# A state-space stage reordered: GpSimd products moved to VectorE, half a projection placed later, outputs as full-array matmuls

## The chip, the core and the metric

The kernel runs on one core of one Trainium2 chip. The metric is device microseconds of one execution, the median of three runs. Matmuls are on TensorE (PE in the profile; its weight loads are PEld), elementwise work on VectorE (DVE), ScalarE (ACT) and GpSimd (POOL); SyncE (SP) issues nearly all DMAs.

## The reference

A two-layer decoder trunk over 512 positions and 1024 channels. Layer 0 is an S5 state-space mixer and a SwiGLU feed-forward network (FFN); layer 1 is latent attention and a second FFN. The change touches only the mixer. Its core, cut to what matters:

```python
def s5_mixer(h, w_in, lam_re, lam_im, log_step, b_re, b_im, c_re, c_im, d_skip, w_glu):
    u = (h @ w_in).reshape(bsz, seq, 64, 16)           # 64 groups of 16 channels
    step = jnp.exp(log_step)[:, None]
    decay = jnp.exp(lam_re * step)
    a_re, a_im = decay * jnp.cos(lam_im * step), decay * jnp.sin(lam_im * step)
    ...                                                # br, bi: input weights scaled by f(a, lambda)
    def scan_sequence(u_seq):                          # x[l] = a * x[l-1] + B u[l], 64 complex states a group
        bu_re = jnp.einsum('gnk,lgk->lgn', br, u_seq)
        bu_im = jnp.einsum('gnk,lgk->lgn', bi, u_seq)
        _, _, xr, xi = lax.associative_scan(combine, (ar_seq, ai_seq, bu_re, bu_im), axis=0)
        return jnp.einsum('gkn,lgn->lgk', cr, xr) - jnp.einsum('gkn,lgn->lgk', ci, xi)
    y = lax.map(scan_sequence, u) + d_skip * u
    z = jax.nn.gelu(y)
    val, gate = jnp.split(z @ w_glu, 2, axis=-1)
    return val * jax.nn.sigmoid(gate)
```

## The kernel before

All fp32 products with full-size weights are made from three fp32r matmuls: each operand is split into a rounded high part (ACT copy) and the rest (DVE subtraction). For weights `weights` does this (DMA into `w`, `wh` on ACT L141, `wl` on DVE L142, two buffers for `w`, three for `wh` and `wl`), for activations `split` does. `mm3` issues the three matmuls (L153, L154, L155).

The mixer (`s5_core`) has four parts.

- **Prologue.** x comes in eight row blocks, `w_in` in eight slabs. Each x block is split (`sh`, `sl`) and squared (`xsq`). `project(0, n)` makes the first half of the projection's columns in four PSUM banks of the kind "x" (96 matmuls), `project(1, n)` the second half in the banks "g" (96 more). Meanwhile DVE, POOL and ACT work out decay, angles and their powers on tiles of 128x32 (`exp_exact`, `turns`, `cmul`), and POOL makes the table `counts`, the tile `DI` and sums of squares.
- **Tiles.** The 512 positions are 128 chunks of 4. Eight tiles t of 8 groups each go through `coefs` (weights W and E for tile t+2, on DVE), `turn_u` and `turn_w` (transposes on PE, copied by ACT into `uT`, `WT`), `rotor` (sines and cosines of whole tiles: `allp` and `near` in PSUM, `whole` on DVE, `Sn`, `Cs` on ACT), `taps` (64x64 matmuls, copied by ACT into `Tb`), `scan` (chunk sums on PE L599, then on DVE: `pc`, `qc`, `z`, two scan instructions L610, `xpc`, `xqc`, and the states `X`), and `outputs`: 16 matmuls with `Tb` (L631) and 64 with E and X (L639) on 128x32 and 64x32 parts of the array, GELU on ACT into `zf`, split into `zh`, `zl`. An fp32 matmul shows as two rows in the trace, a transpose as one.
- **GLU columns in the tiles.** `partial(k)` multiplies tile k's split output with four of the 16 column blocks of `w_glu` (12 matmuls into "g").
- **GLU rest.** In `s5`, for m of 2 to 7, 48 matmuls each, then FFN 0 begins.

The code gives a program order and priorities; a scheduler at build time then fixes one order for each engine, and the chip keeps to it: an instruction that waits holds all those behind it on its engine. PSUM has eight banks; the four "x" banks are handed out in turn, so a new user waits for the readers of the use four before.

Of the kernel before, what the change touches and what calls it, by code (L numbers as in the profile page):

```python
# [88 lines left out]
class Trunk:  # L89
# [207 lines left out]
    def s5_core(self, st):  # L297
# [100 lines left out]
        for t in range(NCT):  # L398
# [5 lines left out]
        tt(counts.rearrange("p a b c -> p (a b) c"), self.c("chunk").unsqueeze(1).broadcast_to([P, 3 * PPC, C]),  # L404
           self.c("pairrow").unsqueeze(2).broadcast_to([P, 3 * PPC, C]), M_, g)
# [43 lines left out]
        for o, x, n, signs in ((ArS, Ar, T + 1, (1.0, -1.0)), (AiN, Ai, T + 1, (-1.0, -1.0)), (GrS, Gr, T, (1.0, 1.0)), (GiS, Gi, T, (-1.0, 1.0))):  # L449
# [5 lines left out]
           self.c("kdelta").unsqueeze(1).broadcast_to([P, 2 * NCT, 32]), M_, g)  # L455
# [14 lines left out]
        Tb = [lp.tile([P, 2, 2, T, 2, 16], F32, name=f"Tb{i}") for i in range(NB)]  # L470
        E2 = [lp.tile([P, 4, 2, T + 1, 2, 16], F32, name=f"E{i}") for i in range(NB)]
# [6 lines left out]
        for z in Tb + E2:  # L478
            g.memset(z, 0.0)
# [3 lines left out]
        def evacuate(q):  # L483

            Us[q] = cp.tile([P, 4 * PPC, T, 16], F32, name="U", bufs=3)
            for i in range(T):
                nc.scalar.activation(out=Us[q][:, :, T - 1 - i, :], in_=ups[q // 2][i][:, (q % 2) * 256:(q % 2 + 1) * 256].rearrange("p (a k) -> p a k", k=16),
                                     func=AF.Copy, scale=rs[:, i:i + 1])

        def coefs(t):  # L490
# [5 lines left out]
            def weigh(o, j, n, re, im):  # L496
                def bb(x):
                    return x.unsqueeze(2).broadcast_to([P, 2 * PPC, n, 16])

# [4 lines left out]
                tt(ma, bb(bc[:, j]), gg(re), M_)
                tt(mb, bb(bc[:, j + 1]), gg(im), M_)
                if o is not None:
                    return tt(o, ma, mb, A_)
                for e in range(2):
                    tt(E2[t % NB][:, :, e, :, e], *(m.rearrange("p (a e) j k -> p a e j k", e=2)[:, :, e] for m in (ma, mb)), A_)

# [3 lines left out]
            weigh(None, 2, T + 1, ArS, AiN)  # L514
            coef[t] = {"W": W}

        def rotor(t):

            allp, near = self.ps("x"), self.ps("x")

            def turns_of(o, j, start, stop):
                nc.tensor.matmul(out=o, lhsT=turned[:, t], rhs=counts[:, j].rearrange("p a b -> p (a b)"), start=start, stop=stop)

            turns_of(allp, 2, True, True)
            whole = cp.tile([P, PPC * C], BF16, name="whole", bufs=1)
            v.tensor_scalar(out=whole, in0=allp, scalar1=MAGIC, scalar2=-MAGIC, op0=A_, op1=A_)
            turns_of(near, 0, True, False)
            nc.tensor.matmul(out=near, lhsT=negident, rhs=whole, start=False, stop=False)
            turns_of(near, 1, False, True)
# [9 lines left out]
        def taps(t):  # L539
# [3 lines left out]
            E = E2[t % NB]  # L543
            kps = [self.ps("x") for _ in range(2)]
            for odd in (1, 0):
                for q in range(2):
                    for c in range(2):
                        for e in range(2):
                            for g2 in range(2):
# [5 lines left out]
                                                 rhs=E[h, 2 * q + c, e, 0:(T if odd else T - 1), e],  # L555
                                                 start=odd == 1 and q == 0 and c == 0, stop=odd == 0 and c == 1, skip_group_check=True)
            for g2 in range(2):
                h = slice(64 * g2, 64 * g2 + 64)
                nc.tensor.matmul(out=kps[g2][:, 0:128].rearrange("p (a u k) -> p a u k", a=2, u=T)[:, :, 0:2, :], lhsT=self.c("places")[h],
                                 rhs=DI[h, 2 * t:2 * t + 2].rearrange("p a (u k) -> p a u k", u=2), start=False, stop=True, skip_group_check=True)  # L560
            for g2 in range(2):
                k4 = kps[g2][:, 0:128].rearrange("p (a u k) -> p a u k", a=2, u=T)
                for e in range(2):
                    for ip in range(2):
                        h = slice(64 * e + 32 * ip, 64 * e + 32 * ip + 32)
                        n = 2 * ip + 2
# [52 lines left out]
        def outputs(t):  # L619

            b = t % NB
            uT, E = states.pop(t), E2[t % NB]
            ps_y = self.ps("x")

            def block(g2, q, j):
                return ps_y[64 * g2 + 32 * q:64 * g2 + 32 * q + 32, j * C:(j + 1) * C]

            for j in range(T):
                for q in range(2):
                    for g2 in range(2):  # L630
                        nc.tensor.matmul(out=block(g2, q, j), lhsT=Tb[t % NB][:, q, g2, j].rearrange("p e k -> p (e k)"), rhs=uT[:, q, g2],  # L631
                                         start=j == 0, stop=False, skip_group_check=True)
            for j in range(T):
                for e in range(2):
                    for c in range(2):
                        for q in range(2):
                            for g2 in range(2):
                                h = slice(64 * g2, 64 * g2 + 64)
                                nc.tensor.matmul(out=block(g2, q, j), lhsT=E[h, 2 * q + c, e, 1 + j].rearrange("p e k -> p (e k)"),  # L639
                                                 rhs=X[b][h, c, 2 * e + q], start=False, stop=e == 1 and c == 1, skip_group_check=True)  # L640
# [18 lines left out]
        for k in range(1, 5):  # L659
            tt(sqs[0], sqs[0], sqs[k], A_, g)  # L660
# [475 lines left out]
```

## Time and profile before

| | |
|---|---|
| median of three runs | 1246.48 us (1244.24 to 1248.38) |
| the profiled execution | 1248.45 us, of which the span of its instructions is 1246.7 us |
| mixer, first instruction to the first FFN matmul | 0 to 276.36 us |
| PE busy in the span | 1190.2 us (95%) |
| DVE, ACT, POOL busy in the span | 673.0, 477.9, 150.4 us |
| mean granted TensorE clock | 0.981 of full speed |

The span runs from the first to the last instruction. Busy shares are means over stages with different limits, so the rows further down cut the span at the borders of the mixer's parts. In a timeline row the first number is the start, the second the time that the merged instructions took; overlapping instructions on PE each show their whole duration, so the spacing of starts tells the pace.

### The profile page before, as it was taken

What the parts mean: (1) busy time and instruction counts of PE and PEld (TensorE: products, weight loads), DVE (VectorE), ACT (ScalarE), POOL (GpSimd) and SP (SyncE); (2) the same over time, 40 slices, a digit from 0 to 9 for tenths busy, and PEclk for the clock granted to TensorE, in tenths of its full rate; (3) what the DMA queues carried; (4) which work ended last, traced back from release to release, by engine and by line L of the source; (5) the groups of instructions that cost most, each with busy time, mean ns of one, the idle gap of its engine ahead of it and who ended that gap; (6) DMA issues with size and microseconds to landing.
All of it is one profiled execution on the core that took longest, in us unless ns stands there. A gap on an engine that the chain in (4) does not pass through costs nothing.

```text
span 1246.7 us, 17562 instructions
## 1 busy us (share of the span) xinstructions
PE 1190.2 (95%) x7160; PEld 964.3 (77%) x7160; DVE 673.0 (54%) x1185; ACT 477.9 (38%) x795; POOL 150.4 (12%) x167
## 2 busy tenths in 40 slices
PE   5978889999999999999999898999999999999998
PEld 4856677888888888888878666666888888888887
DVE  8688895456444444333337777854764444443221
ACT  5464444344333323223336666653342232232210
POOL 4400000002000000000142444342100000000000
PEclk8989899999999999999999899999999999999999
DMA  5201011333333333333232011102333333323331
GB/s 194 89 30 36 10 37 36 118 88 96 104 90 96 101 98 89 93 95 104 85 101 61 27 35 42 52 1 85 88 99 101 92 95 102 102 88 100 121 118 47
DMA packets 31904, 101.09 MB, mean 81 GB/s; under 512 B 3664, under 2 KB 4688, under 8 KB 31824
## 3 DMA queue, kind: packets, MB, share of 16 engines
q1 hardware_dynamic: 31680, 99.97, 26.1%
q8 instruction: 56, 0.92, 0.3%
q14 instruction: 24, 0.20, 0.1%
q10 hardware_dynamic: 144, 0.00, 0.0%
HBM read 97.86 MB, written 2.10 MB: 80 GB/s over the span
## 4 chain that ended last, share of the span: by engine, by line
PE 82%; DVE 13%; ACT 3%; issue 2%; POOL 1%; DMA 0%; DVEq 0%; SPq 0%; ACTq 0%
PE ps_ps L153 19%; PE ps_ps L154 19%; PE ps_ps L155 19%; PE ps_s L942 2%; PE ps_x L154 2%; PE ps_x L155 2%; PE ps_x L153 2%; PE ps_a L153 2%; PE ps_a L155 2%; PE ps_a L154 2%; DVE z L610 1%; PE ps_po L979 1%; PE ps_a L927 1%; PE ps_a L959 1%; PE ps_g L154 1%
## 5 line engine op out<-in xcount | busy, mean ns | idle before, releaser
L141 ACT ACTIVATE wh<-w 128x1024 fp32r<-128x1024 f32 (+3 forms) x193 | 191.0, 992 | 554.5 <-PE ps_ps L154 362.1
L142 DVE TENSOR_TENSOR wl<-w,wh 128x1024 fp32r<-128x1024 f32 (+3 forms) x193 | 222.2, 1152 | 213.4 <-ACT wh L141 213.2
L153 PE MATMUL ps_ps<-fh,wh 128*128 128x512 f32 x704 | 274.2, 390 | 0.0
L155 PE MATMUL ps_ps<-fh,wl 128*128 128x512 f32 x704 | 273.4, 389 | 0.0
L154 PE MATMUL ps_ps<-fl,wh 128*128 128x512 f32 x704 | 273.4, 389 | 0.0
L153 PEld LDWEIGHTS ps_ps<-fh,wh 128*128 128x128 f32 x704 | 132.1, 188 | 28.0 <-issue 0.5
L154 PEld LDWEIGHTS ps_ps<-fl,wh 128*128 128x128 f32 x704 | 132.1, 188 | 27.7 <-issue 0.5
L155 PEld LDWEIGHTS ps_ps<-fh,wl 128*128 128x128 f32 x704 | 132.1, 188 | 27.5
L153 PE MATMUL ps_ps<-ah,wh 128*128 128x512 f32 x352 | 136.9, 389 | 0.0
L154 PE MATMUL ps_ps<-al,wh 128*128 128x512 f32 x352 | 136.9, 389 | 0.0
L155 PE MATMUL ps_ps<-ah,wl 128*128 128x512 f32 x352 | 136.9, 389 | 0.0
L263 POOL TENSOR_TENSOR acc<-acc,sq 128x512 f32<-128x512 f32 x21 | 30.6, 1456 | 580.7 <-ACT sq L258 315.8
L720 DVE TENSOR_TENSOR ut<-ps_ps,rstd 128x512 f32<-128x512 f32 x44 | 30.4, 691 | 127.9 <-PE ps_ps L155 127.9
L155 PEld LDWEIGHTS ps_ps<-ah,wl 128*128 128x128 f32 x352 | 66.1, 188 | 13.8
L154 PEld LDWEIGHTS ps_ps<-al,wh 128*128 128x128 f32 x352 | 66.1, 188 | 13.7
L153 PEld LDWEIGHTS ps_ps<-ah,wh 128*128 128x128 f32 x352 | 66.1, 188 | 13.7
L717 DVE TENSOR_TENSOR gt<-ps_ps,rstd 128x512 f32<-128x512 f32 x44 | 30.4, 691 | 82.8 <-PE ps_ps L155 82.7
L950 POOL TENSOR_SCALAR p<-p,sm 128x128 f32<-128x128 f32 (+2 forms) x48 | 45.7, 955 | 68.8 <-DVE sm L948 61.4
L942 PE MATMUL ps_s<-kT,qT 96*128 96x384 f32 (+3 forms) x128 | 46.3, 465 | 1.6 <-ACT p L947 1.6
L947 ACT ACTIVATE p<-ps_s,mx 128x128 f32<-128x128 f32 (+3 forms) x64 | 33.4, 525 | 29.1 <-DVE mx L945 24.9
L168 ACT ACTIVATE ah<-ut 128x512 fp32r<-128x512 f32 x44 | 27.9, 633 | 31.3 <-DVE ut L721 31.3
L945 DVE TENSOR_REDUCE mx<-ps_s 128x1 f32<-128x128 f32 (+3 forms) x64 | 30.4, 484 | 16.5 <-PE ps_s L943 16.2
(383 smaller groups left out, 1767.7 us busy)
## 6 DMA issues: line engine op xcount, KB each, us to landing
w<-w_gu SPq DMA_DIRECT2D x88, 512.0 KB, 3.5
w<-w_down SPq DMA_DIRECT2D x32, 512.0 KB, 3.5
w<-w_glu SPq DMA_DIRECT2D x12, 512.0 KB, 3.5
w<-w_down SPq DMA_DIRECT2D x16, 384.0 KB, 3.0
w<-w_in SPq DMA_DIRECT2D x7, 512.0 KB, 4.1
w<-w_o SPq DMA_DIRECT2D x6, 512.0 KB, 3.5
x<-xT SPq DMA_DIRECT2D x8, 256.0 KB, 6.9
bc<-ssm_bc SPq DMA_DIRECT2D x8, 256.0 KB, 2.8
```

What stands on the lines that cost most here:

```text
L141: nc.scalar.activation(out=wh[:, c], in_=w[:, c], func=AF.Copy)
L142: nc.vector.tensor_tensor(out=wl[:, c], in0=w[:, c], in1=wh[:, c].bitcast(F32), op=ALU.subtract)
L153: nc.tensor.matmul(out=out, lhsT=lh, rhs=rh, start=start, stop=False)
L154: nc.tensor.matmul(out=out, lhsT=lh, rhs=rl, start=False, stop=False)
L155: nc.tensor.matmul(out=out, lhsT=ll, rhs=rh, start=False, stop=stop)
L263: nc.gpsimd.tensor_tensor(out=acc, in0=acc, in1=sq, op=ALU.add)
L717: v.tensor_tensor(out=gt, in0=pss[0], in1=rstd, op=ALU.mult)
L720: v.tensor_tensor(out=ut, in0=pss[1], in1=rstd, op=ALU.mult)
L942: nc.tensor.matmul(out=ps, lhsT=qT[:, i * P:n], rhs=kT[:, 0:n], start=True, stop=False)
L945: v.reduce_max(out=m1, in_=ps, axis=AX.X, negate=True)
L947: nc.scalar.activation(out=pb, in_=ps, func=AF.Exp, bias=m1, accum_out=s1)
L950: eng.tensor_scalar(out=pb, in0=pb, scalar1=s1, scalar2=None, op0=M_)
```

## The change

The diff, cut to its core:

```diff
+        with tc.high_priority():
             load_x(0)
             load_w(0, 2)
             split_x(0)
...
             split_x(6, 7)
         nc.sync.dma_start(out=self.ct, in_=a["consts"])
...
         counts = sp.tile([P, 3, PPC, C], F32R, name="counts")
-        tt(counts.rearrange("p a b c -> p (a b) c"), self.c("chunk").unsqueeze(1).broadcast_to([P, 3 * PPC, C]),
-           self.c("pairrow").unsqueeze(2).broadcast_to([P, 3 * PPC, C]), M_, g)
+        for j in range(3):
+            for i in range(PPC):
+                nc.scalar.activation(out=counts[:, j, i], in_=self.c("chunk"), func=AF.Copy, scale=self.c("pairrow")[:, PPC * j + i:PPC * j + i + 1])
...
-            tt(q[2], ar, bi, M_, g)
-            tt(q[3], ai, br, M_, g)
+            tt(q[2], ar, bi, M_)
+            tt(q[3], ai, br, M_)
             tt(orr, q[0], q[1], S_)
-            tt(oi, q[2], q[3], A_, g)
+            tt(oi, q[2], q[3], A_)
...
-           self.c("kdelta").unsqueeze(1).broadcast_to([P, 2 * NCT, 32]), M_, g)
+           self.c("kdelta").unsqueeze(1).broadcast_to([P, 2 * NCT, 32]), M_)
...
-            weigh(None, 2, T + 1, ArS, AiN)
-            coef[t] = {"W": W}
+            E = cp.tile([P, 2 * PPC, T + 1, 16], F32, name="E")
+            weigh(E, 2, T + 1, ArS, AiN)
+            for g2 in range(2):
+                h = slice(64 * g2, 64 * g2 + 64)
+                nc.scalar.activation(out=Obd[t % NB][h, :, :, g2], in_=E[h, :, 1:], func=AF.Copy)
+            coef[t] = {"W": W, "E": E}
+
+        def whole_turns(t):
+            allp = self.ps("x")
+            turns_of(t, allp, 2, True, True)
+            rotors[t] = cp.tile([P, PPC * C], BF16, name="whole")
+            v.tensor_scalar(out=rotors[t], in0=allp, scalar1=MAGIC, scalar2=-MAGIC, op0=A_, op1=A_)
...
-            for j in range(T):
-                for q in range(2):
-                    for g2 in range(2):
-                        nc.tensor.matmul(out=block(g2, q, j), lhsT=Tb[t % NB][:, q, g2, j].rearrange("p e k -> p (e k)"), rhs=uT[:, q, g2],
-                                         start=j == 0, stop=False, skip_group_check=True)
...
+            for q in range(2):
+                for g2 in range(2):
+                    nc.tensor.matmul(out=ps_y.rearrange("p (q e j g k) -> p q g e j k", q=2, e=2, j=T, g=2)[:, q, g2], lhsT=uT[:, q, g2],
+                                     rhs=Tb[t % NB][:, q, g2].rearrange("p e j k -> p (e j k)"), start=q == 0 and g2 == 0, stop=False, skip_group_check=True)
+            for q in range(2):
                 for e in range(2):
                     for c in range(2):
+                        nc.tensor.matmul(out=ps_y[:, (2 * q + e) * P:(2 * q + e + 1) * P], lhsT=X[b][:, c, 2 * e + q],
+                                         rhs=Obd[b][:, 4 * q + 2 * c + e].rearrange("p j g k -> p (j g k)"), start=False, stop=c == 1, skip_group_check=True)
+            Y = cp.tile([P, T, PPC, 32], F32, name="Y", bufs=1)
+            nc.scalar.activation(out=Y.rearrange("p j a k -> p a j k"), in_=ps_y.rearrange("p (a j k) -> p a j k", a=PPC, j=T), func=AF.Gelu_apprx_tanh)
+            states[t] = Y
+
+        def turn_y(t):
+            Y = states.pop(t)
+            ps_z = self.ps("x")
+            for j in range(T):
+                nc.tensor.transpose(out=ps_z[:, j * C:(j + 1) * C], in_=Y[:, j].rearrange("p a k -> p (a k)"), identity=ident)
             z = self.pair(t, "z")
-            self.split(z[0], z[1], zf)
+            self.split(z[0], z[1], ps_z)
             zs.append(z)
...
         for k in range(1, 5):
-            tt(sqs[0], sqs[0], sqs[k], A_, g)
+            tt(sqs[0], sqs[0], sqs[k], A_)
...
-        for n in range(4):
-            load_w(4 + n)
-            project(1, n)
         coefs(0)
         turn_u(0)
-        taps(0)
         turn_w(0)
-        rotor(0)
-        scan(0)
-        coefs(1)
-        for t in range(1, 4):
+        for t in range(2):
+            whole_turns(t)
+        rotor(0)
+        taps(0)
+        scan(0)
+        rotor(1)
+        coefs(1)
+        rest(0)
+        for t in range(2, 4):
+            whole_turns(t)
             rotor(t)
         for t in range(NCT):
-            for f, d in ((turn_u, 1), (turn_w, 1), (later_u, 0), (scan, 1), (taps, 1), (outputs, 0), (partial, -1), (coefs, 2)):
+            for f, d in ((turn_u, 1), (turn_w, 1), (scan, 1), (taps, 1), (outputs, 0), (coefs, 2), (turn_y, 0)):
...
+            if t == 0:
+                rest(1)
+                rest(2)
+            if t == 1:
+                rest(3)
+                evacuate(2)
...
+            if t >= 3:
+                for k in range(0 if t == 3 else t - 1, t):
+                    partial(k)
```

`rest(n)` loads slab 4 + n of `w_in` and calls `project(1, n)`. `Obd` holds E for two channel groups side by side, with zeros between, so that one full-array matmul with a state tile X as its weights does what eight small ones did; the result has chunks on the partitions, and `turn_y` turns it back by four transposes before it is split. On POOL only the copies into `phs` and the memsets stay in the mixer. The host's rows of `w_glu` change their order with it.

What the built order makes of it, at three places. First ACT at its very start, where it squares, splits and rounds the first x blocks and weight slabs. Before:

```order
L171 ACT_TABLE_LOAD
L171 ACTIVATE sh_88<-x,smalls 128x512
L346 ACTIVATE xsq<-x 128x512
L141 ACTIVATE wh<-w 128x512 x2
L171 ACTIVATE sh_93<-x,smalls 128x512
L346 ACTIVATE xsq<-x 128x512
L141 ACTIVATE wh<-w 128x1024
L171 ACTIVATE sh_105<-x,smalls 128x512
L346 ACTIVATE xsq<-x 128x512
```

and after the change:

```order
L347 ACT_TABLE_LOAD
L347 ACTIVATE xsq<-x 128x512
L141 ACTIVATE wh<-w 128x512 x2
L171 ACTIVATE sh_88<-x,smalls 128x512
L407 ACTIVATE counts<-ctab 128x128 x12
L409 ACTIVATE negident<-ctab 128x128
L171 ACTIVATE sh_93<-x,smalls 128x512
L347 ACTIVATE xsq<-x 128x512
L141 ACTIVATE wh<-w 128x1024
```

The twelve copies for `counts` and `negident`, which read the constants' DMA (`ctab`), now stand ahead of the second x block `sh_93`; on SP the DMAs of `ctab` and of three `bc` tiles have moved ahead of x blocks 1 to 7 (`ctab`, one `bc`, x1, two `bc`, then the second slab).

Second, ACT ahead of the first scan. `U` is the projection's first half, scaled by the rsqrt `rs`; `wh` 128x1024 is a slab of `w_in`. Before:

```order
L487 ACTIVATE U<-ps_x,rs 128x16x16 x8
L141 ACTIVATE wh<-w 128x1024
L141 ACTIVATE wh<-w 128x512 x2
L487 ACTIVATE U<-ps_g,rs 128x16x16 x4
L141 ACTIVATE wh<-w 128x512
L584 ACTIVATE uT<-ps_x 128x512
```

After:

```order
L489 ACTIVATE U<-ps_x,rs 128x16x16 x8
L517 ACTIVATE Obd_481<-E 64x32x16 x2
L141 ACTIVATE wh<-w 128x1024
L141 ACTIVATE wh<-w 128x512
L591 ACTIVATE uT<-ps_x 128x512
L582 ACTIVATE WT<-ps_x 128x512
L512 ACTIVATE Wz_478<-W 128x8x2x16
L141 ACTIVATE wh<-w 128x512
L517 ACTIVATE Obd_482<-E 64x32x16 x2
L539 ACTIVATE Sn<-ps_x 128x512
L540 ACTIVATE ab<-ps_x 128x512
L541 ACTIVATE Cs<-ab,halfpi 128x512
```

The last slab's `wh` (the first row with 128x1024) stands behind the eight `U` and two `Obd` copies, and a second pair of `Obd` copies stands in front of the first `Sn`, `ab`, `Cs`. On PE, 79 of the second half's 96 projection matmuls stand in front of the first scan matmul (L606, formerly L599), 17 behind it; before it was all 96.

Third, PE around the outputs of tile 0. `ps_x` are the "x" banks, L599/L606 the scan matmuls, L553/L558 the taps. Before:

```order
L599 MATMUL ps_x<-uT,WT 64x128 x8
L573 MATMUL ps_x<-ctab,W 128x128 x4
L631 MATMUL ps_x<-uT,Tb_468 32x128 x16
L639 MATMUL ps_x<-X_472,E_470 32x128 x64
L583 MATMUL ps_x<-ctab,U 128x128 x4
L553 MATMUL ps_x<-E_470,Wz_466 64x64 x8
L553 MATMUL ps_x<-E_470,Wz_466 64x48 x8
L559 MATMUL ps_x<-DI,ctab 128x2x32
```

After:

```order
L633 MATMUL ps_x<-Tb_479,uT 128x8x16 x4
L638 MATMUL ps_x<-Obd_481,X_483 128x128 x8
L590 MATMUL ps_x<-ctab,U 128x128 x4
L580 MATMUL ps_x<-ctab,W 128x128 x4
L648 MATMUL ps_x<-ctab,Y 128x128 x4
L521 MATMUL ps_x<-counts,turned 128x512
L606 MATMUL ps_x<-uT,WT 64x128 x8
L521 MATMUL ps_x<-counts,turned 128x512
L633 MATMUL ps_x<-Tb_480,uT 128x8x16 x4
L638 MATMUL ps_x<-Obd_482,X_484 128x128 x7
L606 MATMUL ps_x<-uT,WT 64x128 x8
```

The 16 and 64 small matmuls have become 4 and 8 full-array ones, and the transposes of `Y` (L648) now stand in front of the next tile's scan matmuls (L606). At the end of the mixer 30 matmuls of `partial(6)` and of the first GLU column block (m = 2) now stand ahead of the last tile's final matmul with X; before it was none.

## Rows read from the trace of the kernel before

**Rows 1.** Busy time of each engine, by stage of the mixer:

```profile
core 0: us, PE busy (x) PEld busy (x) DVE busy (x) ACT busy (x) POOL busy (x), PEclk, DMA share, GB/s
0.00:41.50 41.50, 28.76 (x109) 23.14 (x110) 33.97 (x99) 20.67 (x37) 21.57 (x49) 0.88 0.53 180
41.50:64.60 23.10, 23.10 (x109) 19.29 (x108) 11.60 (x23) 10.00 (x20) 4.49 (x10) 1.00 0.21 63
...
73.00:202.00 129.00, 105.60 (x2014) 86.54 (x2013) 112.40 (x155) 58.08 (x132) 0.00 (x0) 0.91 0.08 23
202.00:276.40 74.40, 74.35 (x433) 61.92 (x434) 32.44 (x51) 29.37 (x37) 0.00 (x0) 1.00 0.33 99
```

**Rows 2.** What DVE waited for from 73 to 202 us (total, times, longest):

```profile
DVE pc L367 <- PE ps_x L599: 6.4, 3, 6.0
DVE whole L526 <- PE ps_x L528: 5.4, 2, 2.7
DVE W L367 <- PE ps_x L573: 3.6, 2, 2.0
```

**Rows 3.** DVE in order of time, tiles 0 to 7:

```profile
73.02 0.69 DVE L367 TENSOR_TENSOR pc<-ps_x,Cs 128x512 f32<-128x512 f32 x1
...
85.79 0.69 DVE L367 TENSOR_TENSOR pc<-ps_x,Cs 128x512 f32<-128x512 f32 x1
...
99.67 0.82 DVE L367 TENSOR_TENSOR wb<-bc,AiN 128x640 f32<-128x640 f32 x1
100.40 0.68 DVE L367 TENSOR_TENSOR pc<-ps_x,Cs 128x512 f32<-128x512 f32 x1
101.00 0.68 DVE L367 TENSOR_TENSOR qc<-ps_x,Sn 128x512 f32<-128x512 f32 x1
...
200.72 1.28 DVE L367 TENSOR_TENSOR X<-xpc,xqc 128x508 f32<-128x508 f32 x2
```

**Rows 4.** PE in order of time: last tile's outputs, first FFN matmul:

```profile
202.05 3.48 PE L639 MATMUL ps_x<-X,E 64*32 64x128 f32 x120 [0.18 <-DVE X L367]
...
276.36 0.62 PE L153 MATMUL ps_ps<-fh,wh 128*128 128x512 f32 x2
```

**Rows 5.** DVE in order of time, prologue:

```profile
17.69 2.73 DVE L228 TENSOR_SCALAR ts<-txl 128x32 f32<-128x32 f32 x1
...
22.34 0.74 DVE L172 SCALAR_TENSOR_TENSOR sl<-x,smalls,sh 128x512 fp32r<-128x512 f32 x1
23.00 0.18 DVE L230 SCALAR_TENSOR_TENSOR ts<-txl,ts 128x32 f32<-128x32 f32 x1
23.10 0.18 DVE L227 TENSOR_TENSOR tf<-tf,tn 128x32 f32<-128x32 f32 x1
...
26.58 1.21 DVE L142 TENSOR_TENSOR wl<-w,wh 128x1024 fp32r<-128x1024 f32 x1
27.72 0.17 DVE L191 TENSOR_SCALAR tn<-tp 128x32 f32<-128x32 f32 x1
```

**Rows 6.** POOL in order of time, prologue:

```profile
17.18 3.20 POOL L367 TENSOR_TENSOR counts<-ctab 128x1536 fp32r<-128x1536 f32 x1
```

**Rows 7.** ACT in order of time, before the tiles:

```profile
18.23 0.29 ACT L407 ACTIVATE negident<-ctab 128x128 bf16<-128x128 f32 x1
...
49.62 3.03 ACT L487 ACTIVATE U<-ps_x,rs 128x256 f32<-128x256 f32 x8 [4.57 <-DVE rs L187]
52.48 1.11 ACT L141 ACTIVATE wh<-w 128x1024 fp32r<-128x1024 f32 x1
```

**Rows 8.** PE in order of time: phase transposes, and the outputs of one tile:

```profile
41.49 1.03 PE L462 MATMUL ps_g<-ctab,phs 128*128 128x128 f32 x8
42.36 0.50 PE L666 MATMUL ps_g<-ctab,xsq 128*128 128x1 f32 x4
...
124.59 1.08 PE L631 MATMUL ps_x<-uT,Tb 128*32 128x128 f32 x32
125.60 3.70 PE L639 MATMUL ps_x<-X,E 64*32 64x128 f32 x128
```

More of the change, by code (lines that the diff above doesn't have):

```diff
@@ L469, in s5_core @@
         Wz = [lp.tile([P, 2 * PPC, 5, 16], F32, name=f"Wz{i}") for i in range(NB)]
-        Tb = [lp.tile([P, 2, 2, T, 2, 16], F32, name=f"Tb{i}") for i in range(NB)]
-        E2 = [lp.tile([P, 4, 2, T + 1, 2, 16], F32, name=f"E{i}") for i in range(NB)]
+        Tb = [lp.tile([P, 2, 2, 2, T, 16], F32, name=f"Tb{i}") for i in range(NB)]
+        Obd = [lp.tile([P, 2 * PPC, T, 2, 16], F32, name=f"Obd{i}") for i in range(NB)]
         X = [lp.tile([P, 2, PPC, C], F32, name=f"X{i}") for i in range(NB)]
@@ L477, in s5_core @@
             g.memset(RH[b][:, :, 0:1], 0.0)
-        for z in Tb + E2:
+        for z in Tb + Obd:
             g.memset(z, 0.0)
@@ L505, in weigh @@
                 tt(mb, bb(bc[:, j + 1]), gg(im), M_)
[L506 to L509, printed above, removed]
+                tt(o, ma, mb, A_)
             W = cp.tile([P, 2 * PPC, T, 16], F32, name="W", bufs=1)
@@ L513, in coefs, with turns_of @@
             nc.scalar.activation(out=Wz[t % NB][:, :, 1:5:2], in_=W[:, :, 0:1, :].broadcast_to([P, 2 * PPC, 2, 16]), func=AF.Copy)
-            weigh(None, 2, T + 1, ArS, AiN)
-            coef[t] = {"W": W}
-        def rotor(t):
[L519 to L529, printed above, removed]
+            E = cp.tile([P, 2 * PPC, T + 1, 16], F32, name="E")
[4 more added lines that the diff above has]
+            coef[t] = {"W": W, "E": E}
+        def turns_of(t, o, j, start, stop):
+            nc.tensor.matmul(out=o, lhsT=turned[:, t], rhs=counts[:, j].rearrange("p a b -> p (a b)"), start=start, stop=stop)
+        def whole_turns(t):
[3 more added lines that the diff above has]
+            v.tensor_scalar(out=rotors[t], in0=allp, scalar1=MAGIC, scalar2=-MAGIC, op0=A_, op1=A_)
+        def rotor(t):
+            near = self.ps("x")
+            turns_of(t, near, 0, True, False)
+            nc.tensor.matmul(out=near, lhsT=negident, rhs=rotors[t], start=False, stop=False)
+            turns_of(t, near, 1, False, True)
             Sn = cp.tile([P, PPC, C], F32, name="Sn", bufs=4)
@@ L633, in outputs @@
-            for j in range(T):
+            for q in range(2):
+                for g2 in range(2):
+                    nc.tensor.matmul(out=ps_y.rearrange("p (q e j g k) -> p q g e j k", q=2, e=2, j=T, g=2)[:, q, g2], lhsT=uT[:, q, g2],
+                                     rhs=Tb[t % NB][:, q, g2].rearrange("p e j k -> p (e j k)"), start=q == 0 and g2 == 0, stop=False, skip_group_check=True)
+            for q in range(2):
                 for e in range(2):
                     for c in range(2):
[L636 to L640, printed above, removed]
```

74 lines of the change are left out of this document (37 added, 37 removed).

## Prediction

> **What bounds the kernel now.** I read the stages of the mixer first, then who waits in them, then the timelines at their borders. PE is 95% busy over the span, but the stages differ [rows 1]. From 202 us on it is busy without a gap (74.35 of 74.40 us), and from 41.5 to 64.6 us too, with the second half of the projection. Over the tiles, 73 to 202 us, it is not what holds: 105.6 of 129 us, and its clock is granted at 0.91 there, against 1.00 before and after. DVE is busy for 112.4 of these 129 us, and nearly all the rest are three named waits for PE, 15.4 us [rows 2]. Where DVE doesn't wait, one tile follows the other at 100.40 - 85.79 = 14.6 us [rows 3], and that is the plain sum of its instructions. So the tiles are bound by DVE plus its waits, and they start only at 73.02 us, with the first `pc` [rows 3], since PE works the second projection half off first. The prologue up to 41.5 us has DVE at 34.0 and PE at 28.8 of 41.5 us [rows 1]. Everything behind 276.36 us, the first FFN matmul [rows 4], is the same code in both kernels, and PE has no gap ahead of it: what the mixer saves there is saved at the end.
>
> I therefore cut the mixer in three: (A) to the first `pc`, 73.02 us; (B) from there to the last `X`, 200.72 + 1.28 = 202.0 us, so 129.0 us; (C) from there to 276.36 us, 74.4 us.
>
> **A, the start.** After the change PE has 79 of the 96 second-half matmuls ahead of the first scan, so the filler is only 17 of them; what brings the scan forward is that DVE, not PE, paces this stage. I add up what stands on DVE ahead of its first `pc` in the built order: 21 instructions of 512 elements at 0.60 us (the spacing of `pc` and `qc` [rows 3]), 6 of 640 at 0.75 (spacing 0.73, duration 0.82), 8 x splits at 0.66 and 7 slab remainders at 1.14 (spacings [rows 5]), 6 of 128 elements at 0.3 (an estimate between those of 32 and 512), and 95 of 32 or 64 elements or fewer at 0.15, between their spacing of 0.10 and their duration of 0.18 [rows 5]: 12.6 + 4.5 + 5.3 + 8.0 + 1.8 + 14.2 = 46.4 us. This has the former POOL work in it (products, four sums of squares, `DI`), some 6 us of DVE. In return DVE's small instructions are no longer stretched: `ts`, 32 elements, took 2.73 us [rows 5] while POOL ran `counts`, 3.20 us from 17.18 [rows 6], against 0.18 for the same kind later. The first `wl` can start at about 6.2 us, once x block 0 and the first half slab have landed and ACT has worked on them. 6.2 + 46.4 = 52.6.
>
> Then the waits. ACT does 12 `counts` copies of 128x128 and `negident` ahead of `sh_93`; at `negident`'s 0.29 us [rows 7] or somewhat less that is 3.2 to 3.5 us in the way, and ACT reaches the last x block about 21 us in, ahead of DVE's place for it: 0.3 us of wait. Slabs 4 and 5 need a free `w` buffer and a DMA: 0.7 us. The last slab's `wh` stands behind `rs`, eight `U` (3.03 us [rows 7]) and two `Obd` copies (about 1.1, from the spacing of `U` for twice the elements); by `rs` at 44 us it is done near 49.2, while DVE wants it at 46.2: 3.0 us. Last, ACT copies the second `Obd` pair before `Sn`, `ab`, `Cs`: 1.4 us. 52.6 + 5.4 = 58.0 us. PE is just in time: first half done at about 32 us, 79 x 0.227 = 17.9 us, and some 4 us of transposes, phases and taps, so 55 us. **A: 73.0 - 58.0 = 15.0 us less.** Bounds: 54 us without the two ACT waits (19 less); 63 us if the constants and `bc` tiles (1.1 MB) ahead of x cost their 3 us in full and the small instructions 0.18 each (10 less).
>
> **B, the tiles.** DVE's work there is nearly unchanged: one more `zl` and one more `wl` (0.6 each), and six times one E of 640 elements in place of two of 320 (under 0.1 less each). From 129.0 - 15.4 = 113.6 I get 114.3 us. The waits: 5.4 us of `whole` for L528 came of one buffer and of `partial` standing between its users; `whole_turns` runs earlier with two buffers, so I drop them. The 6.0 us of the last `pc` came of taps and `partial` matmuls ahead of L599; in the code the scan's matmuls now come ahead of the taps, but the built order keeps the last tile's taps first, so part of it stays, as do the 3.6 us of `W` for its transposes. New ones: `zl` waits for outputs, GELU, four transposes and `zh` in a row, and the transposes hold the PE behind them. I take 8 us, about half of today's. **B: 122.3, 6.7 us less.** Bounds: none at all, 14.7 less; today's 15.4, 0.7 more.
>
> What the outputs cost PE: today 32 rows L631 and 128 rows L639 are 1.08 + 3.70 = 4.7 us a tile [rows 8]. After, 24 full-array fp32 rows and four transposes. No such matmul is in the trace; transposes of that shape follow at (42.36 - 41.49)/8 = 0.11, and fp32 weight loads of 128 columns with a one-column matmul at about 0.12 (0.50/4) [rows 8]. Bounds 0.11 and 0.23 (both in full): 2.6 to 5.5 us; I take 0.13, nearer the transposes because loads overlap matmuls, so 3.1 + 0.5 = 3.6 us, about a microsecond under today's, beside DVE either way.
>
> The Trainium skill speaks against this part: "TensorE: Matmul & The Clock Gate", Part 3 (packing small matmuls), has small tiles of the array run at the same time, up to 10.6 times faster, and the change gives up eight at a time. The row shows how much of it arrives: 128 rows in 3.70 us is 29 ns each, so the 8-fold packing carries 8-fold instructions. The same page's LDWEIGHTS section gives columns/1.2 ns, 107 ns for 128; by it the 24 rows are an estimated 2.6 us, and C would be 0.4 us shorter.
>
> **C, behind the last X.** Today PE then runs the rest of L639 (3.48 us [rows 4]) and 312 fp32r matmuls: (276.36 - 202.05 - 3.48)/312 = 0.227 each. After, 30 of them stand ahead of the last output matmuls: 282 x 0.227 = 64.0, plus 16 rows at 0.13 and the transposes, 2.6, plus 1.0 as PE gets to that place late (those 30 need a slab split only 5 us before). **C: 67.6, 6.8 us less.** Bounds 7.8 and 4.
>
> **The sum.** 15.0 + 6.7 + 6.8 = 28.5 us. The profiled execution took 1248.45 us, 1.97 above the median; against itself 1219.95, against the median 1246.48 - 28.5 = 1218.0 us. What hides the edits costed at nothing (POOL's memsets, `bc` DMAs, `Obd` copies in the tiles) is ACT's and POOL's idle time: ACT is busy 58 of 129 us [rows 1] and gets about 1 us a tile more.
>
> **Rivals.**
> 1. Prologue late on PE: if the first half of the projection still ends at 41.5 us (x blocks late behind the constants), the 79 matmuls bring the first `pc` to 41.5 + 1 + 17.9 + 4 = 64.5, and the gain falls to 22 us: 1224.5. For it: six DMA transfers change places and ACT starts 3 us later on block 1. Against: today's end comes of DVE being late, not of the data.
> 2. PE becomes the bound of the tiles: at 0.23 a row outputs take 6.0 us a tile, taps, scan, transposes and phases about 6 and `partial` 2.7, together 14.7 of DVE's 15.8; each hiccup then shows. With 12 us of new waits: 1230. The Trainium skill's packing rule above points the same way.
> 3. Slower: `turn_y`'s transposes stand ahead of the next tile's scan matmuls, wait for GELU, and GELU on ACT stands behind the copy `RH`, which waits for DVE's scan. One such wait today is 6.0 us (the longest `pc` wait [rows 2]). At 6 us in each of eight tiles B grows by 40 us more than I have: 1258. It decides from 8 + 28.5/8 = 4.6 us of wait a tile. Against: two X buffers let DVE run a tile ahead, as the undisturbed 14.6 us spacing shows.
> 4. The change does not do what it says: the filler is small, as counted; if DVE's prologue is then also slower by what POOL gave up, A gives 9 and the sum is 22, inside the range.
>
> **Chances.** Forecast (gain 17 to 40): 0.78. Rivals 1 and 4 fall partly into it; below it, 4 to 17, mostly rival 2: 0.12. More than 40 (no waits at all): 0.05. Rival 3 or nothing: 0.05. A measurement of this kernel tells about 0.3%, 3.7 us, from no change. Faster 0.95, same 0.02, slower 0.03. The extremes of the terms together would give 5 to 42 us; leaving out a tenth at either end, 15 to 40: 1206 to 1231.
>
> **What would show it.** A: first `pc` at 54 to 63 us, no DVE instruction of 32 elements over 1 us, a DVE wait for the last slab's `wh`. B: last `X` at 176 to 186 us, no `whole` wait, DVE busy 113 to 115 of the stage. C: first FFN matmul near 248 us. Wrong: a `pc` wait of several us in every tile, L638 rows over 0.2 us apart, or a granted clock under 0.85 over the tiles.

## The result, and the profile after

The changed kernel takes 1228.49 us (median of 4 runs, 1227.18 to 1228.76), the kernel before beside it 1247.11: a ratio of 0.9855, 95% interval 0.9842 to 0.9868, so 18.1 us less (16.5 to 19.7). The forecast was 28.5 us less, with a range of 17 to 40; the measured gain lies near its lower end. The profiled execution took 1228.52 us with a span of 1226.7 us, 20.0 less than before.

The stages of the mixer, cut at the same events as in [rows 1]:

```profile
core 0: us, PE busy (x) PEld busy (x) DVE busy (x) ACT busy (x) POOL busy (x), PEclk, DMA share, GB/s
0.00:41.50 41.50, 33.36 (x148) 27.01 (x149) 33.56 (x130) 28.00 (x55) 11.53 (x40) 1.00 0.56 189
41.50:58.17 16.67, 16.67 (x170) 13.48 (x170) 10.30 (x17) 11.42 (x24) 1.13 (x2) 1.00 0.31 80
58.17:184.10 125.93, 109.10 (x1116) 92.42 (x1120) 112.74 (x150) 68.56 (x155) 0.00 (x0) 0.85 0.10 28
184.10:255.38 71.28, 70.56 (x320) 57.84 (x318) 31.26 (x50) 26.74 (x35) 0.00 (x0) 1.00 0.31 96
sum 255.38, PE 229.69 PEld 190.76 DVE 187.85 ACT 134.72 POOL 12.66; mean PE 57.42 PEld 47.69 DVE 46.96 ACT 33.68 POOL 3.17
```

| | forecast | measured |
|---|---|---|
| A, to the first `pc` | 73.0 to 58.0 | 73.0 to 58.2 |
| B, to the last `X` | 129.0 to 122.3 | 129.0 to 125.9 |
| C, to the first FFN matmul | 74.4 to 67.6 | 74.4 to 71.3 |
| behind it | the same | 970.3 to 971.3 (968.4 to 972.2 in the kernels below) |

A is met. B and C each miss by 3.6 or 3.7 us. In the tiles the granted clock is 0.85, not 0.91, and DVE waits nearly as long as before, for other things than in [rows 2]:

```profile
DVE pc L368 <- PE ps_x L606: 8.8, 5, 2.9
DVE wl L142 <- ACT wh L141: 3.2, 2, 1.7
DVE W L368 <- PE ps_x L580: 2.1, 1, 2.1
DVE zl L169 <- ACT zh L168: 0.3, 1, 0.3
```

DVE in order of time (start, duration, and in brackets the wait ahead of it), the rows that answer to [rows 3, 5]:

```profile
5.00 0.69 DVE L142 TENSOR_TENSOR wl<-w,wh 128x512 fp32r<-128x512 f32 x1 [4.13 <-ACT wh L141]
...
47.21 1.23 DVE L142 TENSOR_TENSOR wl<-w,wh 128x1024 fp32r<-128x1024 f32 x1 [3.19 <-ACT wh L141]
...
58.17 0.69 DVE L368 TENSOR_TENSOR pc<-ps_x,Cs 128x512 f32<-128x512 f32 x1 [2.08 <-PE ps_x L606]
...
93.65 0.69 DVE L368 TENSOR_TENSOR pc<-ps_x,Cs 128x512 f32<-128x512 f32 x1 [2.12 <-PE ps_x L606]
...
113.07 0.69 DVE L368 TENSOR_TENSOR pc<-ps_x,Cs 128x512 f32<-128x512 f32 x1 [1.05 <-PE ps_x L606]
...
131.97 0.69 DVE L368 TENSOR_TENSOR pc<-ps_x,Cs 128x512 f32<-128x512 f32 x1 [2.86 <-PE ps_x L606]
...
170.84 1.29 DVE L368 TENSOR_TENSOR X<-xpc,xqc 128x508 f32<-128x508 f32 x2
...
182.82 1.28 DVE L368 TENSOR_TENSOR X<-xpc,xqc 128x508 f32<-128x508 f32 x2
```

PE in order of time, in the tiles and at their end (an answer to [rows 4, 8]):

```profile
83.24 0.65 PE L648 MATMUL ps_x<-ctab,Y 128*128 128x128 f32 x4 [2.68 <-ACT Y L641]
85.01 0.62 PE L521 MATMUL ps_x<-counts,turned 128*128 128x512 f32 x1 [1.12 <-ACT uT L591]
85.56 1.97 PE L606 MATMUL ps_x<-uT,WT 64*64 64x128 f32 x16
...
102.20 1.90 PE L558 MATMUL ps_x<-E,Wz 64*64 64x64 f32 x32 [3.06 <-ACT uT L591]
...
130.83 1.09 PE L606 MATMUL ps_x<-uT,WT 64*64 64x128 f32 x16
...
150.87 3.21 PE L638 MATMUL ps_x<-Obd,X 128*128 128x128 f32 x16
...
166.59 1.95 PE L638 MATMUL ps_x<-Obd,X 128*128 128x128 f32 x16
...
177.55 1.95 PE L638 MATMUL ps_x<-Obd,X 128*128 128x128 f32 x16
...
180.66 0.47 PE L153 MATMUL ps_x<-zh,wh 128*128 128x512 f32 x1
...
187.36 0.39 PE L638 MATMUL ps_x<-Obd,X 128*128 128x128 f32 x2
...
255.38 0.62 PE L153 MATMUL ps_ps<-fh,wh 128*128 128x512 f32 x2
```

A pattern shows here. PE waits 2.7 us for GELU (`Y`), then runs the 16 scan rows in 1.97 us; at full clock 16 such rows take 1.09 us, as at 130.83. The second half of that scan stands behind the outputs, and `pc` waits 2.12 us at 93.65. The end shows the term of C that failed. Tile 6's X is complete at 172.1, and PE comes to it at 177.55; the last tile's is complete at 184.10, and PE comes to it at 187.36, since the 30 matmuls ahead started only at 180.66.

### The profile page after: what moved, and what is told of

Read it like the earlier page. It is cut to its first block, busy times and chain, and to the rows that moved or that the text cites. A ratio compares the mean times of both kernels' runs of the same rounds, so it can differ in the third digit from the quotient of the medians.

```text
span 1226.7 us, 15533 instructions
## 1 busy us (share of the span) xinstructions
PE 1182.0 (96%) x6133; PEld 959.8 (78%) x6136; DVE 664.2 (54%) x1194; ACT 489.2 (40%) x821; POOL 137.2 (11%) x149
## 4 chain that ended last, share of the span: by engine, by line
PE 83%; DVE 9%; ACT 4%; issue 2%; POOL 1%; DMA 1%; SPq 0%; DVEq 0%; ACTq 0%
PE ps_ps L155 20%; PE ps_ps L154 20%; PE ps_ps L153 19%; PE ps_s L965 2%; PE ps_x L153 2%; PE ps_x L155 2%; PE ps_x L154 2%; PE ps_a L153 2%; PE ps_a L154 2%; PE ps_a L155 2%; DVE wl L142 1%; PE ps_x L638 1%; PE ps_g L153 1%; PE ps_x L606 1%; PE ps_po L1002 1%
```

## The experiments

All ratios are to the kernel before, on the same chip; a difference of two kernels is the difference of their ratios times 1247 us. The cuts are those of each kernel's own profiled execution, in us; "To tile 3's `pc`" counts from the first `pc`, and each of the next two columns from the cut before it. PE idle is the time to the first FFN matmul less PE's busy time in it. The profiled execution of partials sooner took 1225.77 us, 4.1 more than its kernel's median; those of packed outputs and outputs only took 3.4 and 3.3 us less than theirs.

| kernel | ratio, 95% interval | first `pc` | to tile 3's `pc` | from there to last `X` | from there to first FFN matmul | PE busy, idle | clock in the tiles |
|---|---|---|---|---|---|---|---|
| before | 1 | 73.0 | 49.6 | 79.4 | 74.4 | 238.1, 38.2 | 0.91 |
| changed | 0.9855 (0.9842 to 0.9868) | 58.2 | 54.9 | 71.0 | 71.3 | 229.7, 25.7 | 0.85 |
| prologue only | 0.9961 (0.9949 to 0.9973) | 65.6 | 49.6 | 77.4 | 74.4 | 233.8, 33.2 | 0.91 |
| outputs only | 0.9945 (0.9928 to 0.9962) | 70.9 | 49.8 | 72.4 | 72.9 | 229.7, 36.4 | 0.79 |
| half in front | 0.9855 (0.9842 to 0.9868) | 65.2 | 48.6 | 69.2 | 71.6 | 224.5, 30.2 | 0.93 |
| packed outputs | 0.9937 (0.9925 to 0.9949) | 58.9 | 55.5 | 74.8 | 74.3 | 236.4, 27.1 | 0.88 |
| turn_y later | 0.9847 (0.9834 to 0.9860) | 58.9 | 50.9 | 70.0 | 74.1 | 224.9, 29.1 | 0.83 |
| partials sooner | 0.9791 (0.9778 to 0.9804) | 62.1 | 47.7 | 70.2 | 73.0 | 226.1, 26.9 | 0.86 |
| RH on POOL | 0.9841 (0.9827 to 0.9854) | 60.1 | 54.3 | 67.9 | 74.1 | 223.2, 33.2 | 0.89 |
| outputs twice | 0.9932 (0.9919 to 0.9946) | 61.7 | 54.8 | 74.4 | 75.1 | 236.9, 29.1 | 0.91 |
| dummies | 0.9803 (0.9789 to 0.9818) | 58.9 | 49.6 | 66.5 | 74.2 | 228.6, 20.5 | 0.91 |
| small dummies | 0.9821 (0.9802 to 0.9840) | 59.5 | 51.1 | 70.3 | 71.4 | 226.1, 26.3 | 0.90 |
| sooner and dummies | 0.9813 (0.9794 to 0.9832) | 58.1 | 49.8 | 70.3 | 73.9 | 230.6, 21.5 | 0.87 |
| rotor behind U | 0.9836 (0.9812 to 0.9861) | 61.9 | 51.1 | 70.5 | 72.6 | 228.8, 27.3 | 0.85 |

### The parts of the change

**Prologue only**, in the kernel before:

```diff
+        with tc.high_priority():
             load_x(0)
...
-        tt(counts.rearrange("p a b c -> p (a b) c"), ..., M_, g)
+                nc.scalar.activation(out=counts[:, j, i], in_=self.c("chunk"), func=AF.Copy, scale=...)
...
-            tt(q[2], ar, bi, M_, g)
+            tt(q[2], ar, bi, M_)
```

> The kernel before with only the prologue's part of the change: high priority for the x and w_in work, no POOL products, counts on ACT; projection, tiles and outputs as before. My theory (DVE paces the prologue, PE follows it): PE ends the first half near 31.6 us as in the changed kernel, the whole second half is 96 x 0.227 = 21.8 us, transposes, phases and taps 4 to 6, so the first pc stands at 58 to 61 us; the tiles stay at 129 us and the rest at 74, so the gain is 12 to 15 us: 1232 to 1235. Rival (it is the filler, not the prologue, that brings the tiles forward): first pc at 66 us or later, gain at most 7: 1240 or more.

Measured: 4.9 us less (3.4 to 6.4), first `pc` at 65.6 us. That is the rival's side: the prologue alone brings the first scan 7.4 us forward, not 12 to 15.

**Half in front**, in the changed kernel:

```diff
+        for n in range(4):
+            load_w(4 + n)
+            project(1, n)
         coefs(0)
...
-        rest(0)
...
-                rest(1)
-                rest(2)
```

> The changed kernel with all 96 matmuls of the second half of the projection ahead of the first scan, as before the change. My theory (only 17 matmuls were moved, 3.9 us): first pc at 61 to 62 us, the tiles as in the changed kernel or up to 2 us shorter, since PE has less between the scans: 1228 to 1232. Rival (the filler carries a good part of the gain): 1236 or more.

Measured: the same time as the changed kernel. The first `pc` comes 7.0 us later (more than the 17 matmuls' 3.9 that I counted, as the transposes, turns and taps move behind them too), and the tiles are 8.1 us shorter, not up to 2. DVE's waits in the tiles are 6.1 us here:

```profile
DVE wl L142 <- ACT wh L141: 2.7, 1, 2.7
DVE pc L368 <- PE ps_x L606: 2.7, 3, 1.5
DVE W L368 <- PE ps_x L580: 0.7, 1, 0.7
```

So the filler gives the tiles an earlier start that they lose again before the last X.

**Packed outputs**, in the changed kernel (the outputs, `Tb`, `E2` and the rows of `w_glu` as before):

```diff
-                        nc.tensor.matmul(out=ps_y[:, (2 * q + e) * P:(2 * q + e + 1) * P], lhsT=X[b][:, c, 2 * e + q], rhs=Obd[b][...], ...)
+                                nc.tensor.matmul(out=block(g2, q, j), lhsT=E[h, 2 * q + c, e, 1 + j]..., rhs=X[b][h, c, 2 * e + q], ...)
...
-(outputs, 0), (coefs, 2), (turn_y, 0)):
+(outputs, 0), (coefs, 2)):
```

> The changed kernel with the outputs of the kernel before: 16 + 64 small matmuls, no block-diagonal copies on ACT, no transposes of Y, z split straight from the GELU's tile. Theory 1 (the tiles lose their time because PE stands behind the transposes that wait for GELU, and then runs the next scan at the lower clock): from first pc to last X 121 us or less in place of 125.9, no wait of PE of several us for ACT, granted clock over the tiles above 0.88, mixer over by 251 us: 1223 or less. Theory 2 (the transposes' wait only takes the place of another one, and the small matmuls cost PE a microsecond a tile more): 125 to 128 us for the tiles, 1228 to 1232.

**Outputs only**, in the kernel before: the same lines the other way round, with `(turn_y, 0)` behind `(outputs, 0)`.

> The kernel before with the outputs part of the change alone (full-array matmuls, block-diagonal copies on ACT, transposes of Y, the new row order of w_glu; two bc buffers in place of three, to make room); prologue, projection and the turns as before. Theory (as the kernel with packed outputs was about 10 us slower than the changed one, the outputs are worth 7 to 10 us by themselves, since PE's time in the tiles is on the path): 1237 to 1240. Rival (their worth comes only with the tiles' earlier start, where PE is short; before it DVE covers them): 1243 to 1248. My prediction's own step would give the rival.

Measured: packed outputs make the changed kernel 0.9937 - 0.9855 = 0.0082, 10.2 us slower, which neither theory had; the outputs alone make the kernel before 6.9 us faster (4.7 to 9.0). Both say that the outputs are worth 7 to 10 us; in the profiled execution with the outputs alone, 2.1 us of the lead lie ahead of the first `pc`, and that kernel also has two `bc` buffers in place of three. The stages with packed outputs and with the outputs alone, tiles and sum of the mixer:

```profile
58.91:189.26 130.35, 111.64 (x2029) 91.89 (x2031) 111.67 (x155) 61.48 (x142) 0.00 (x0) 0.88 0.08 24
...
sum 263.57, PE 236.44 PEld 194.69 DVE 189.30 ACT 128.04 POOL 12.80; mean PE 78.81 PEld 64.90 DVE 63.10 ACT 42.68 POOL 4.27
```

```profile
70.94:193.14 122.20, 98.04 (x1085) 85.28 (x1085) 110.86 (x148) 64.55 (x144) 0.00 (x0) 0.79 0.09 25
...
sum 266.08, PE 229.72 PEld 192.30 DVE 194.25 ACT 130.25 POOL 25.21; mean PE 76.57 PEld 64.10 DVE 64.75 ACT 43.42 POOL 8.40
```

PE's busy time moves with them: 238.1 to 229.7 us by the outputs alone, 229.7 to 236.4 by taking them back, while DVE's busy time in the tiles stays at 111 to 113 us. By itself that is no proof, since busy time grows at a lower clock too: half in front and RH on POOL, with 0.93 and 0.89 over the tiles, have 5.2 and 6.5 us less of it than the changed kernel with 0.85, and the same time. The next kernel is the direct test.

With the prologue's 4.9 us this accounts for 12 to 15 of the 18.1 us. The place of the projection by itself does not give the other 3 to 6, as half in front shows; the turns called earlier, the later `partial`, or the parts acting together may. No kernel here tests those alone.

**Outputs twice**, in the changed kernel:

```diff
-                    for c in range(2):
+                    for c in (0, 1, 0, 1):
```

> The changed kernel with each of the 8 state matmuls of a tile's outputs done twice, so that the states count double in the output. My prediction's step (outputs lie beside DVE, so PE's time in the tiles is nearly free): 16 more rows a tile, 1.95 us at full clock, 15.6 in all, of which only the last tile's 2 are on the path: 1229 to 1232. Rival (PE's work is on the path of most tiles): 10 to 16 us more, 1238 to 1245.

Measured: 0.0077, 9.6 us slower than the changed kernel, with 1238.88 us in the rival's range. The 128 more rows are 15.6 us at 1.95/16 = 0.12 each. Between the two profiled executions 3.5 of 10.6 us lie ahead of the first `pc`, where the kernels do the same work, and 7.1 behind it. So some 45 to 60% of this work on PE shows in the time.

### What holds the tiles

**Turn_y later**, in the changed kernel:

```diff
-(scan, 1), (taps, 1), (outputs, 0), (coefs, 2), (turn_y, 0)):
+(scan, 1), (taps, 1), (turn_y, -1), (outputs, 0), (coefs, 2)):
...
-            ab = cp.tile([P, PPC, C], F32, name="ab", tag="Y", bufs=1)
+            ab = cp.tile([P, PPC, C], F32, name="ab", bufs=1)
```

> The changed kernel with the transposes of Y one tile later (ahead of the next tile's outputs), and a buffer of its own for ab, which shared Y's. Theory 1 (as for the packed outputs): pc waits fall from 8.8 us to under 4, first pc to last X 121.5 us or less in place of 125.9, 1223 to 1225; if z of tile 6 then comes late for the first GLU block, up to 2 us of it are given back behind the last X. Theory 2 (PE is held by PSUM banks that ACT reads late, wherever the transposes stand): the waits come back on W, zl or pc, 125 to 127 us, 1227 to 1230.

Measured: the `pc` waits fall from 8.8 to 4.3 us and the tiles to 120.9, as theory 1 has it, but 2.8 us come back behind the last X and `wl` waits 6.3 us; the time is not separable from the changed kernel's.

**RH on POOL**, in the changed kernel:

```diff
-            nc.scalar.activation(out=RH[b][:, :, 1:]..., in_=rho[...]..., func=AF.Copy)
+            g.tensor_copy(out=RH[b][:, :, 1:]..., in_=rho[...]...)
```

> The changed kernel with the copies RH on POOL instead of ACT. Theory (GELU stands behind RH on ACT, RH waits for DVE's scan, and so the transposes of Y hold PE): PE's waits for Y fall from 5.2 us to under 3 and the tiles by 2 to 4 us: 1224 to 1226. Rival (POOL beside DVE costs DVE more than that, as counts did in the prologue before): DVE's instructions in the tiles get longer, busy over 115 us, 1229 or more.

Measured: the waits for `Y` fall to 3.7 us, DVE's busy time in the tiles grows from 112.7 to 114.0. The tiles are 3.7 us shorter, but the first `pc` comes 1.9 us later and 2.8 us come back behind the last X, and the time is not separable from the changed kernel's. Neither effect is worth much.

**Partials sooner**, in the changed kernel:

```diff
-            Us[q] = cp.tile([P, 4 * PPC, T, 16], F32, name="U")
+            Us[q] = cp.tile([P, 4 * PPC, T, 16], F32, name="U", bufs=3)
...
                 evacuate(2)
+                evacuate(3)
...
-            if t >= 3:
-                for k in range(0 if t == 3 else t - 1, t):
+            if t >= 2:
+                for k in range(0 if t == 2 else t - 1, t):
```

> The changed kernel with the second half's last U evacuated one tile sooner (a third U buffer, and two bc buffers in place of three to make room) and partial(0) and partial(1) one tile sooner, so that partial runs once a tile from tile 2 on, not three times at tile 3. Theory (what holds the tiles is PE's block of partial matmuls and the late U copies around tile 3, at 102 to 118 us; an earlier start only waits longer for it): tile 3's first pc goes from 113.1 us to 106 to 109, the waits of DVE in the tiles from 14.4 us to 10 or less, last X at 178 to 180 us, 1222 to 1225. Rival (it is ACT's block of table load, sines and cosines for tiles 4 and 5, from 98 to 108 us): tile 3's pc stays at 111 to 113, 1227 to 1230.

Measured: 1221.65 us, 0.0064 or 8.0 us faster than the changed kernel. From the first `pc` to tile 3's it takes 47.7 us, not 54.9. This is the best median, 26 us under the kernel before; the dummies below are not separable from it.

**Dummies**, and **small dummies** (16 columns in place of 512), in the changed kernel:

```diff
             ps_z = self.ps("x")
+            for _ in range(4):
+                turns_of(t, ps_z, 2, True, True)
             for j in range(T):
```

> The changed kernel with four more 512-column matmuls a tile, right behind the outputs, into the bank that the transposes of Y will overwrite: work with no result, 8 x 4 x 0.227 = 7.3 us at full clock. Theory (the tiles lose time because PE, after a wait, does the next scan at the lower clock): granted clock over the tiles above 0.90 in place of 0.85, tiles not longer than 126 us, 1226 to 1230. Rival (PE's work counts, whatever its clock): tiles 4 to 8 us longer, 1232 to 1237.

> The changed kernel with four matmuls of 16 columns where the dummies of 512 columns stood. The built order is nearly that of the kernel with the 512-column dummies, but the work added is small. Theory (the dummies gained 6 us because they keep PE busy over its wait, and so its clock up): the granted clock over the tiles is 0.85 to 0.88 again, the tiles 121 us or more, 1226 to 1230. Rival (they gained by the other order of transposes, outputs and partial matmuls that the scheduler makes with them): clock as it may, the tiles at 118 us or less, 1221 to 1224.

Measured: more work on PE, and 6.5 us faster than the changed kernel, as my theory of the clock had it. But the small dummies, in nearly the same order, are 4.2 us faster too, and what the work adds to that (0.0018, 2.2 us) is inside the intervals. So most of the gain does not need the work. Whether it is the order's or the clock's is not settled: with the small dummies the granted clock over the tiles is 0.90 as well, where the theory had 0.85 to 0.88, and the tiles take 121.5 us, where the rival had 118 or less. In both orders the copy `uT` of tile 3 stands ahead of a table load and the sines of tile 4; in the changed kernel it stood behind. ACT in order of time, first the changed kernel, then with small dummies:

```profile
98.14 1.28 ACT L539 ACT_TABLE_LOAD   x1
99.44 0.60 ACT L539 ACTIVATE Sn<-ps_x 128x512 f32<-128x512 f32 x1
...
101.55 0.60 ACT L591 ACTIVATE uT<-ps_x 128x512 f32<-128x512 f32 x1
```

```profile
97.47 0.59 ACT L591 ACTIVATE uT<-ps_x 128x512 f32<-128x512 f32 x1
...
100.53 1.28 ACT L539 ACT_TABLE_LOAD   x1
101.83 0.60 ACT L539 ACTIVATE Sn<-ps_x 128x512 f32<-128x512 f32 x1
```

**Sooner and dummies**, both edits at once:

> Both of the faster versions in one: partial from tile 2 on with the earlier U copies, and the four 512-column dummies ahead of the transposes of Y. Theory (both fill the same idle stretches of PE, so the gains of 6.8 and 5.8 us overlap in the main): 1218 to 1222. Rival (two causes, the block of partial matmuls at tile 3 and the clock, each with its own price): the gains add to 1215 or 1216.

Measured: 0.9813, no gain over either. The two gains do not add, as if both edits took the same loss away.

**Rotor behind U**, in the changed kernel, to test that place alone:

```diff
                     f(t + d)
+                if f is turn_u and t in (2, 4):
+                    rotor(t + 2)
+                    rotor(t + 3)
...
-            if t in (1, 3):
-                rotor(t + 3)
-                rotor(t + 4)
```

> The changed kernel with rotor(4) and rotor(5), and rotor(6) and rotor(7), called in the next tile behind turn_u, so that at tile 3 the transposes of U, their copy uT and the transposes of Y stand ahead of the turns' matmuls, the table load and the sines; up to that place PE's built order is the changed kernel's, row for row. Theory (what the dummies of any size gained is this order: in the changed kernel uT of tile 3 is copied at 101.6 us, behind a table load and a sine, and PE waits 3.1 us for it, then runs slower): uT at 96 to 98 us, no wait of PE of 3 us for it, tile 3's first pc at 106 to 109 us in place of 113.1, 1222 to 1225. Rival (the gain came of the later tiles or of the first ones, or of the clock): tile 3's pc comes sooner, but the last X stays at 182 to 185 us, 1227 to 1230.

ACT in order of time, and DVE at tile 3's first `pc`:

```profile
100.95 0.60 ACT L591 ACTIVATE uT<-ps_x 128x512 f32<-128x512 f32 x1
...
104.15 1.28 ACT L539 ACT_TABLE_LOAD   x1
```

```profile
113.04 0.69 DVE L368 TENSOR_TENSOR pc<-ps_x,Cs 128x512 f32<-128x512 f32 x1
```

Measured: inconclusive in the time (0.9836, interval 0.9812 to 0.9861). Tile 3's first `pc` stands at 113.04 us, where the changed kernel has 113.07 and I expected 106 to 109. By its own start, this execution's first `pc` being 3.7 us later, tile 3 comes 51.1 us behind it, 3.8 less than in the changed kernel; `uT` has moved ahead of the table load, and PE's wait of 3.06 us for it is gone there.

## Why the prediction was right, and where it was not

**A was right in its sum, with errors that cancel.** The first `wl` came at 5.0, not 6.2; DVE's work was 33.56 + 10.30 = 43.9, not 46.4; the waits were 58.2 - 5.0 - 43.9 = 9.3, not 5.4. The wait for the last slab's `wh` was named and sized rightly (3.2 for 3.0). In place of 1.4 us for `Cs` there were 2.1 us for the first scan's matmuls, and 1.0 more behind the last slab. "DVE, not PE, paces this stage" was half the truth: the prologue alone gave 7.4 of the 14.8 us, and the place of the projection the other 7.

**B: the mis-sized term is the waits of DVE: 8 us taken, 14.4 measured** (DVE's work was 111.5, 2.8 less than my 114.3). I dropped the waits of `whole` rightly, and put the new ones on `zl`, which waits 0.3 us. They are on `pc`, `wl` and `W`. What I left out is that A and B are not separable. With the filler moved back, A is 7.0 us longer, B 8.1 shorter, and DVE's waits are 6.1 us, below what I took. The table shows where the loss lies: from the first `pc` to tile 3's it is 54.9 us in the changed kernel, and 47.7 to 51.1 in all kernels that put something else in order there, while the three others (packed outputs, RH on POOL, outputs twice) stay at 54.3 to 55.5, and before had 49.6. The rows point to the late `uT` as one cause of these 5 us, but that is argued, not shown: the direct test shortened that stretch by 3.8 us only as counted from its own later start, and its total can't be told from no gain. Two kernels that recover (turn_y later, partials sooner) leave the sines ahead of `uT`. So there is more than one way past the loss, and which of the waits of PE at tiles 1 to 3 is needed for it stays open.

**C: the mis-sized term is "plus 1.0 as PE gets to that place late"**: it was 187.36 - 184.10 = 3.3. From there it took 68.0 us, 67.3 of work and 0.7 of waiting, for my 66.6. PE had already come to tile 6's outputs 5.4 us late.

**The outputs were costed at nothing, and that step failed.** Each matmul's price was right (24 rows, 1.00 + 1.88 us by the spacing of starts at full clock, 0.12 each for my 0.13), but "beside DVE either way" was wrong: by two kernels the outputs are worth 7 to 10 us, the largest part that was measured by itself, and by a third some 45 to 60% of more work in them shows in the time. Behind the last X, PE has no gap, so whatever PE has not done by then comes on top, and in the tiles `pc` waits for matmuls that stand behind the outputs. The Trainium skill's packing rule ("TensorE: Matmul & The Clock Gate", Part 3), which spoke against this part, does not decide here: 128 packed rows took 3.70 us [rows 8], 16 full ones take 1.95. The missing gain of the outputs and the unkept part of A's gain cancelled in part, and so the sum came within 8.5 us by the profiled executions, 10.4 by the ratio. That it came so near is in part luck.

**The rivals.** None won as written. Rival 1 fell, since the first half of the projection ended near 31.8 us, not 41.5:

```profile
31.37 0.40 PE L155 MATMUL ps_x<-wh,sl 128*128 128x512 f32 x1
```

Rival 2 (PE becomes the bound) had the right place and nearly the right time, 1230, but not by its price of 0.23 us a row. Rival 3's mechanism is there (waits for `Y` of 5.2 us in all) at a tenth of its price. Rival 4's reason fell: the changed kernel's small DVE instructions take 0.2 us. Of the named signs, the first FFN matmul came at 255.4 us, not near 248, and the granted clock over the tiles, 0.85, stood on the bound given for being wrong.

## What to carry to other kernels

Where one engine runs without a gap to the end of a stage, add up its busy and idle time over the whole stage before saying that its work is hidden beside another engine: here PE's busy time fell by 8.4 us with the outputs alone, and the mixer by 10.3. Busy time also grows when the clock falls, so check the sum by doing the work twice. An earlier start is worth what the next late thing leaves of it, so forecast the stages together, with the buffers and copies that tie them. When an experiment adds instructions, a scheduler also gives a new order; run the same order with almost no work in it before believing in the work.

## What the runs showed of the hardware

Kernels with nearly the same prologue work had their first `pc` at 58.1 to 58.9 us (five of them), at 59.5 and 60.1 (small dummies, RH on POOL), or at 61.7 to 62.1 (outputs twice, rotor behind U, partials sooner). Two waits go with it. PE waited 0.4 to 0.7 us ahead of the phase transposes in the first five, 1.6 and 1.5 in the next two, and 1.9 to 2.2 in the late three; a slab remainder of DVE waited 0.5 to 0.8, then 1.8 and 1.9, then 1.8 to 2.3. In the late three alone the granted clock was lower behind that wait (0.83 to 0.88 from 40 to 50 us, against 1.00 in the other seven). What makes the waits longer is not shown. Here the kernel with the outputs done twice:

```profile
38.84 0.61 PE L464 MATMUL ps_g<-ctab,phs 128*128 128x128 f32 x2 [2.12 <-POOL phs L402]
```

```profile
30.00:40.00 10.00, 7.88 (x42) 6.49 (x41) 7.56 (x42) 5.42 (x12) 6.18 (x24) 0.95 0.33 113
40.00:50.00 10.00, 10.00 (x43) 8.41 (x42) 6.04 (x14) 7.58 (x19) 4.08 (x11) 0.88 0.09 29
```

So against the changed kernel 1.4 us more of waiting on PE went with 3.5 us at the first `pc`.

In the tiles of the changed kernel PE waited 2.24 us, and soon after it worked for 9.5 us on end at the lower of the clock's two levels (1.2 of 2.4 GHz):

```profile
67.03 0.66 PE L580 MATMUL ps_x<-ctab,W 128*128 128x128 f32 x4 [2.24 <-ACT ab L540]
```

```profile
68.50:78.00 9.50, 9.50 (x118) 9.34 (x118) 8.71 (x14) 5.46 (x16) 0.00 (x0) 0.50 0.21 57
```

The lower clock lengthens the rows: in the changed kernel 16 L638 rows took 1.95 us at full clock (from 166.59) and 3.21 us where the mean granted clock was 0.58 (from 150.87). Yet the best two kernels have 0.86 and 0.91 over the tiles and differ by less than their intervals: the mean clock did not order these kernels.
